# The norm of the memory tokens in two passes: row sums first with one raw tile for each block, then a second load whose rows ScalarE scales, and the norm's weight applied where the turned rows leave PSUM

## The chip, the core and the metric

One NeuronCore of a Trainium2 chip runs the whole program. The time is the device's time for one execution in microseconds (us), and of several runs the median counts. PE is TensorE (matmuls; PEld are its weight loads), ACT is ScalarE, DVE is VectorE, POOL is GpSimd, and SP is the queue of the sync engine, which here issues nearly all DMA transfers.

## The reference, cut to what matters

One encoder layer: a token mixer with two groups of attention heads, a cross-attention into 256 memory tokens, and an MLP. The part that changes is the norm of the memory tokens ahead of the cross-attention's keys and values:

```python
def rmsnorm(x, g):
    y = xf * lax.rsqrt(jnp.mean(xf * xf, axis=-1, keepdims=True) + EPS) * g
...
mem_n = rmsnorm(mem, g_mem_kv[l])          # mem: 256 x 1024
k = (mem_n @ w_mk).reshape(B, M, MEM_HEADS, MEM_HEAD_DIM)
v = (mem_n @ w_mv).reshape(B, M, MEM_HEADS, MEM_HEAD_DIM)
```

## The kernel before

Every product runs as three matmuls of split operands: an operand is cut into a high part (`hi`, rounded by an ACT copy) and a low part (`lo`, the difference, by DVE or POOL), and `mm3` (lines 193 to 195) adds hi x hi, lo x hi and hi x lo in PSUM.

The attention phase starts about 60 us into the span. A planner, the class `Flow`, writes the order of the instructions of every engine while the program is built: it keeps six streams of PE steps and queues of small jobs for ACT ("S"), DVE ("V"), POOL ("G") and SP ("D"), each with an assumed cost, and at each point takes the first stream whose next step is ready by its own clock. On the chip each engine then runs its list strictly in this order. The streams are, by priority: the value products of the heads (`pv`, line 766), the transposes of probabilities (`ptr`, line 723), the scores (`sc..`/`sf..`, lines 650 and 651), side steps, row statistics, and last the filler, which projects the q, k and v of later head pairs (n = 0 to 7; tiles `q_0`, `q_1`, `k_0`, ...). The filler of pair n+1 may start only when the tiles of an older pair are free, that is when that pair's scores are all done. So at each change of pair the filler can run out shortly before it may go on.

A unit of scores for 128 queries goes in pieces, here of 384 and 256 columns: two matmuls into one of two PSUM banks (tag `s`), then a custom DVE instruction (line 654) that adds the bias and takes the row minimum, which also frees the bank. ACT takes the exponent (line 663), POOL normalises (line 666), PE transposes, ACT and DVE split the result into `phl` (lines 732 and 729).

Weights come through a ring of three raw 128 x 1024 tiles (tag `wraw`): class `Stock` lists the blocks in the order of their use, loads one as soon as a raw tile is free, and splits it on ACT (line 461) and POOL or DVE when a place for the split weight is free. Two entries in that list belong to the memory tokens. At "norm", placed ahead of q of pair 5, `mem_norm` takes all three raw tiles: one for the norm's weight spread over 128 partitions, two for the blocks of memory rows; each block is squared and summed on ACT (line 931), its root taken on POOL (lines 934 and 935), scaled by root and weight in one DVE instruction (line 937) and stored to DRAM (`md`). At "mem", ahead of k of pair 7, `mem_loads` loads the two normed blocks again (`memn`). `side_steps` then turns them on PE in four groups of four 128 x 128 transposes (`tr_mem`), and each group leaves PSUM by one ACT copy (`mT_hi`, line 915) and one DVE subtraction (`mT_lo`, line 912). The memory's key product `mk` is the next filler.

Of the kernel before, what the change touches and what calls it, by code (L numbers as in the profile page):

```python
# [14 lines left out]
F32 = mybir.dt.float32  # L15
# [7 lines left out]
P = 128  # L23
S = 1024
# [10 lines left out]
def f(ap):  # L35
    return ap.bitcast(F32)
# [99 lines left out]
def build(ctx, tc, nc, out, t):  # L136
# [105 lines left out]
    nc.vector.memset(o1024, 1.0 / 1024.0)  # L242
    bfgt = const.tile([8, 1], F32, name="bfgt")
    gcol = const.tile([P, KC], F32, name="gcol")

    od = [[dr.tile([P, HT], F32, name=f"od{k}_{h}") for h in range(2)] for k in range(KC)]
    x1d = [dr.tile([P, D], F32, name=f"x1d{b}") for b in range(TB)]
    x2d = [dr.tile([P, D], F32, name=f"x2d{b}") for b in range(TB)]
    rd = dr.tile([8, 768], F32, name="rd")
    md = [dr.tile([P, D], F32, name=f"md{b}") for b in range(2)]  # L250
    cd = dr.tile([8, S], F32, name="cd")
    td = {k: [dr.tile([P, 2, HT], F32, name=f"{k}d{i}") for i in range(2)] for k in ("T1", "T2", "T3", "T4")}

# [121 lines left out]
    def raw_tile(name):  # L375
        return wp.tile([P, D], F32, tag="wraw", bufs=3, name=name)
# [22 lines left out]
    class Stock:  # L399
# [3 lines left out]
        def __init__(self):  # L403
            self.blocks = []
            for n, (kind, pr) in enumerate(ORDER):
                if n == 5:
                    self.blocks.append("norm")
                b = (0 if kind == "f" else 8) + pr
                self.blocks.append((("q", n), t["w_qk"][b], [P, KC, P]))
                if n > 3:  # L410
                    self.blocks.append((("v", n), t["w_v"][n - 4], [P, KC, P]))
                if n == 7:
                    self.blocks.append("mem")
                self.blocks.append((("k", n), t["w_qk"][b + 4], [P, KC, P]))
# [71 lines left out]
        def pump(self):  # L486

            while self.to_load:
                if isinstance(self.to_load[0], str):
                    n = 3 if self.to_load[0] == "norm" else 2  # L490
                    if not free["raw"].ready(n):
                        break
                    for _ in range(n):
                        free["raw"].take()
                    (mem_norm if self.to_load.pop(0) == "norm" else mem_loads)()
                    break
                if not free["raw"].ready():
                    break
                free["raw"].take()
                key = self.to_load[0][0]  # L500
                self.load()
                flow.put("D", flow.now, 0.55, lambda: None, lambda at, k=key: seen.__setitem__(("raw", k), at + 4.2))
# [370 lines left out]
    def side_steps():  # L873
# [23 lines left out]
        for k in range(0, KC, 2):  # L897
# [8 lines left out]
                    nc.tensor.transpose(tr[:, j, q, :], mem_in[q][:, (k + j) * P:(k + j + 1) * P], ident)  # L906
            src = tr.rearrange("p a q b -> p a (q b)")
            i, o = k // mT.per, k % mT.per
            dh, dl = mT.h[i][:, o:o + 2, :], mT.l[i][:, o:o + 2, :]

            def lo(at, src=src, dh=dh, dl=dl, k=k):
                flow.put("V", at, 0.7, lambda: nc.vector.tensor_sub(dl, src, f(dh)),
                         lambda end: (free["tr"].give(end), seen.__setitem__(("mT", k), end)), 1)

            flow.put("S", flow.end, 0.6, lambda src=src, dh=dh: nc.scalar.activation(dh, src, AF.Copy), lo, 1)
        for _ in range(2):
            free["raw"].give(flow.end)


    def mem_norm():  # L920

        g = raw_tile("g_mem_kv")
        nc.sync.dma_start(g, t["g_mem_kv"].to_broadcast([P, D]))
        for b in range(2):
            xt = raw_tile(f"mem{b}")
            nc.sync.dma_start(xt, t["mem"][b * P:(b + 1) * P, :])
            r, ss = (small.tile([P, 1], F32, tag=k, bufs=8, name=f"{k}_mem{b}") for k in ("rstd", "ss"))

            def square(xt=xt, ss=ss, b=b):
                junk = p1.tile([P, D], BF16, tag="phl", bufs=2, name=f"junkm{b}")  # L930
                nc.scalar.activation(junk, xt, AF.Square, scale=1.0 / 32.0, accum_out=ss)

            def root(r=r, ss=ss):
                nc.gpsimd.tensor_scalar(r, ss, EPS, None, op0=ALU.add)
                nc.gpsimd.tensor_tensor(r, r, mhalf[:, 0:1], op=ALU.pow)

            scale = lambda xt=xt, r=r: nc.vector.scalar_tensor_tensor(xt, xt, r, g, op0=ALU.mult, op1=ALU.mult)
            store = lambda xt=xt, b=b: nc.sync.dma_start(md[b], xt)
            flow.chain(flow.now + 6 + b, [("S", 1.1, square), ("G", 0.9, root), ("V", 1.3, scale), ("D", 0.55, store)],
                       lambda at, b=b: [free["raw"].give(at) for _ in range(1 + b)] and seen.__setitem__(("md", b), at))  # L940

    mem_in = []

    def mem_loads():
        for b in range(2):
            xt = raw_tile(f"memn{b}")
            nc.sync.dma_start(xt, md[b])
            mem_in.append(xt)
        seen["mem"] = flow.now + 6

    def memory_steps(keep):
        for nb in range(KC):
# [896 lines left out]
    with tc.manual_schedule():  # L1849
# [116 lines left out]
            nc.scalar.activation(rrows[:, th, :], tr.rearrange("p a b -> p (a b)"), AF.Copy)  # L1966
        nc.sync.dma_start(bfgt, t["b_fgt"])
        nc.sync.dma_start(gcol, t["g_heads"])

        def scaled(th, kc):  # L1970
            x = xT[th][kc // 2][:, kc % 2, :]
# [806 lines left out]
def _layout(i):  # L2778
    import numpy as np

    def a(x):
        return np.ascontiguousarray(np.asarray(x, dtype=np.float32) if not isinstance(x, np.ndarray) else x)
# [6 lines left out]
    def parts(w, ranges):  # L2789
# [25 lines left out]
        "w_ff2q": a(i["w_ff2"][0].reshape(2, 2, 4, 2, P, 2, 2, 256)[1].transpose(4, 2, 5, 0, 3, 1, 6).reshape(2, 4, 2, P, D)),  # L2815
        "w_ff2": a(i["w_ff2"][0].reshape(2, 8, 2, P, 2, HT).transpose(0, 4, 1, 3, 2, 5).reshape(4, 8, P, D)),
        "g_mem_pre": a(i["g_mem_pre"].reshape(KC, P).T),
        **{k: i[k] for k in ("g_mix_post", "g_mem_kv", "g_mem_post",
                             "g_ff_pre", "g_ff_post")},
    }  # L2820

# [13 lines left out]
```

## Time and profile before

| | |
|---|---|
| median of 3 runs | 1450.36 us (1448.18 to 1451.93) |
| span of the profiled execution | 1448.0 us |
| PE busy | 1436.0 us (99%) |
| PEld busy | 1223.0 us (84%) |
| DVE busy | 1127.7 us (78%) |
| ACT busy | 871.1 us (60%) |
| POOL busy | 373.9 us (26%) |
| granted TensorE clock | 1.000 over the span, its upper level of 2.4 GHz |

The span runs from the first instruction to the last; nothing else of the profiled execution's own time is recorded, and the three runs lie between 0.2 and 3.9 us above it. A matmul's busy time reaches beyond the start of the next one, since matmuls are pipelined. So an engine that is "99% busy" can hide short stalls, and they are read from the starts: in a stretch without waits a matmul over 512 columns starts 0.23 us after the one before it, over 384 columns 0.17 us, over 256 columns 0.12 us. What a start is late by those steps is a stall, whether the view counts it as idle time or not.

### The profile page before, as it was taken

Reading aid. Unit: us, or ns where it says so; the run is one execution under the profiler, and the core shown is the slowest. Engines: PE = TensorE matmul, PEld = TensorE weight load, DVE = VectorE, ACT = ScalarE, POOL = GpSimd, SP = SyncE. Lnnn points to the kernel's source line nnn. Section 1 sums busy time; section 2 is a strip of 40 time slices with the busy share of each in tenths; the row PEclk is TensorE's granted clock in tenths of the full one; section 3 lists DMA queues with packets and bytes.
Section 4 is the critical chain, followed back from the end, with each engine's and each line's share of the span. In section 5 each row is a group of like instructions: output and inputs, shape, how many; then the busy total and the mean of one; then the engine's idle time right before and its main releaser. Section 6 shows DMA issues by size and latency. Waiting matters only on the chain. (4 is left out here: it accounts for less than half of the span.)

```text
span 1448.0 us, 21869 instructions
## 1 busy us (share of the span) xinstructions
PE 1436.0 (99%) x7505; PEld 1223.0 (84%) x7505; DVE 1127.7 (78%) x1918; ACT 871.1 (60%) x1509; POOL 373.9 (26%) x472
## 2 busy tenths in 40 slices
PE   9999999999999999999999999999999999999998
PEld 8988888888889888888888888888888888888886
DVE  6788787867677856879788787996666866789897
ACT  6567676766677845885566565445555555555553
POOL 1145565645454310211113511003322000000003
PEclk9999999999999999999999999999999999999999
DMA  7143424442415585542144637775455996786785
GB/s 278 49 121 98 120 70 139 150 124 65 106 54 153 172 291 205 192 157 88 44 133 173 219 130 242 260 262 185 167 178 179 315 344 238 259 283 229 275 290 204
DMA packets 109439, 262.12 MB, mean 181 GB/s; under 512 B 12280, under 2 KB 30720, under 8 KB 109328
## 3 DMA queue, kind: packets, MB, share of 16 engines
q1 hardware_dynamic: 109184, 260.47, 54.0%
q8 instruction: 59, 0.97, 0.3%
q14 instruction: 52, 0.43, 0.1%
q10 hardware_dynamic: 144, 0.26, 0.1%
HBM read 186.70 MB, written 65.59 MB: 174 GB/s over the span
## 5 line engine op out<-in xcount | busy, mean ns | idle before, releaser
L729 DVE TENSOR_TENSOR phl<-ptr,phl 128x512 fp32r<-128x512 f32 (+1 forms) x152 | 92.3, 615 | 30.9 <-ACT phl L732 29.7
L732 ACT ACTIVATE phl<-ptr 128x512 fp32r<-128x512 f32 (+1 forms) x152 | 79.6, 539 | 49.4 <-PE ptr L723 47.7
L2471 ACT ACTIVATE whif<-ra 128x1024 fp32r<-128x1024 f32 x45 | 47.6, 1059 | 76.8 <-PE fx L194 34.8
L2606 POOL TENSOR_SCALAR rf<-sf 128x1 f32<-128x1 f32 x7 | 7.0, 1004 | 316.0 <-ACT jf L2587 315.8
L766 PE MATMUL pv<-phl,vs 128*128 128x512 f32 (+1 forms) x304 | 85.9, 367 | 0.4 <-DVE phl L729 0.4
L2473 DVE TENSOR_TENSOR wlof<-ra,whif 128x1024 fp32r<-128x1024 f32 x45 | 55.0, 1222 | 35.9 <-ACT whif L2471 35.8
L193 PE MATMUL fx<-vhif,whif 128*128 128x512 f32 x168 | 65.6, 390 | 0.0
L194 PE MATMUL fx<-vlof,whif 128*128 128x512 f32 x168 | 65.6, 390 | 0.0
L195 PE MATMUL fx<-vhif,wlof 128*128 128x512 f32 x168 | 65.4, 389 | 0.0
L766 PEld LDWEIGHTS pv<-phl,vs 128*128 128x128 f32 x304 | 54.7, 188 | 10.5 <-DVE phl L729 1.4
L780 POOL TENSOR_TENSOR o<-o 64x256 f32<-64x256 f32 x64 | 47.8, 747 | 51.8 <-DVE o L778 35.3
L2322 POOL TENSOR_TENSOR sc<-wf,wf 128x512 f32<-128x512 f32 x8 | 12.7, 1581 | 177.4 <-DMA wf<-in_w_ff 177.4
L1545 POOL TENSOR_SCALAR mp<-mp,mst 128x256 f32<-128x256 f32 x32 | 24.6, 775 | 125.1 <-DVE mst L1544 85.7
L193 PE MATMUL k<-hT_hi,whik 128*128 128x512 f32 x128 | 53.2, 416 | 0.0
L193 PE MATMUL q<-hT_hi,whiq 128*128 128x512 f32 x128 | 51.7, 404 | 0.0
L778 DVE TENSOR_TENSOR o<-pv,o 64x512 f32<-64x512 f32 x64 | 43.9, 686 | 9.7 <-ACT o L783 8.7
L193 PE MATMUL yw<-whiwo,yT_hi 128*128 128x512 f32 x128 | 50.6, 395 | 0.0
L195 PE MATMUL k<-hT_hi,wlok 128*128 128x512 f32 x128 | 50.3, 393 | 0.0
L194 PE MATMUL k<-hT_lo,whik 128*128 128x512 f32 x128 | 50.3, 393 | 0.0
L194 PE MATMUL yw<-wlowo,yT_hi 128*128 128x512 f32 x128 | 50.2, 392 | 0.0
L195 PE MATMUL q<-hT_hi,wloq 128*128 128x512 f32 x128 | 50.1, 392 | 0.0
L194 PE MATMUL q<-hT_lo,whiq 128*128 128x512 f32 x128 | 50.1, 392 | 0.0
(786 smaller groups left out, 5267.6 us busy)
## 6 DMA issues: line engine op xcount, KB each, us to landing
wg<-in_w_ff SPq DMA_DIRECT2D x48, 512.0 KB, 6.1
ra<-gd SPq DMA_DIRECT2D x40, 512.0 KB, 3.8
wf<-in_w_ff SPq DMA_DIRECT2D x38, 512.0 KB, 3.8
wi<-in_w_ff2q SPq DMA_DIRECT2D x28, 512.0 KB, 5.5
gd<-s SPq DMA_DIRECT2D x32, 256.0 KB, 2.7
gd<-g SPq DMA_DIRECT2D x25, 256.0 KB, 2.8
wrawq<-in_w_qk SPq DMA_DIRECT2D x8, 512.0 KB, 4.5
wrawk<-in_w_qk SPq DMA_DIRECT2D x8, 512.0 KB, 3.7
```

Source lines behind the costliest of these rows:

```text
L193: nc.tensor.matmul(ps, lh, rh, start=start, stop=False, skip_group_check=more)
L194: nc.tensor.matmul(ps, lh, rl, start=False, stop=False, skip_group_check=more)
L195: nc.tensor.matmul(ps, ll, rh, start=False, stop=stop, skip_group_check=more)
L729: flow.put("V", at, 0.7, lambda: nc.vector.tensor_sub(pl[:, live, :], tr[:, live, :], f(ph[:, live, :])), done)
L732: flow.put("S", flow.end, 0.6, lambda ph=ph, tr=tr, live=live: nc.scalar.activation(ph[:, live, :], tr[:, live, :], AF.Copy), split)
L766: nc.tensor.matmul(pv[:, :, qs_, :], v, hl[:, :, hs, :], start=c == 0 and turn == 0, stop=last)
L778: flow.put("V", at, 0.7, lambda: nc.vector.tensor_add(o2[own], pv[own, :, :, ::step], o2[own]), lambda end: (free["pv"].give(end), flow.pu ...
L780: free["pv"].give(end), flow.put("G", end, 0.8, lambda: nc.gpsimd.tensor_add(o2[own, 0], o2[own, 0], o2[own, 1]), store)))
L1545: mul = lambda st=st, pr=pr: nc.gpsimd.tensor_scalar(pr, pr, st[:, 2:3], 1.0, op0=ALU.mult, op1=ALU.mult)
L2322: eng.tensor_sub(sc[:, k1], r0[:, k0], r1[:, k0])
L2471: nc.scalar.activation(ah, ra, AF.Copy)
L2473: nc.vector.tensor_sub(al, ra, f(ah))
```

## The change

The "norm" entry stands twice in the list, ahead of q of pairs 4 and 5, and takes one raw tile each time. Such an entry loads one block of memory rows, squares it in place on ACT with the row sums going to a column of a small constant tile `rkv`, and takes the root there on POOL. The DVE multiplication, the load of the spread weight and the stores to `md` are gone. At "mem" both blocks are loaded again from the input, and ACT scales each in place by its root column. The weight is loaded as 128 x 8 columns (`gkv`) near the start. When turned rows leave PSUM, memory channels lie on partitions, so the weight is a column there: each group of transposes now leaves in two halves, each by an ACT copy scaled by a weight column and a DVE `scalar_tensor_tensor` with the same column, 128 x 256 apiece.

```diff
             for n, (kind, pr) in enumerate(ORDER):
-                if n == 5:
+                if n in (4, 5):
                     self.blocks.append("norm")
...
-                    n = 3 if self.to_load[0] == "norm" else 2
+                    n = 1 if self.to_load[0] == "norm" else 2
...
-            dh, dl = mT.h[i][:, o:o + 2, :], mT.l[i][:, o:o + 2, :]
-
-            def lo(at, src=src, dh=dh, dl=dl, k=k):
-                flow.put("V", at, 0.7, lambda: nc.vector.tensor_sub(dl, src, f(dh)),
-                         lambda end: (free["tr"].give(end), seen.__setitem__(("mT", k), end)), 1)
-
-            flow.put("S", flow.end, 0.6, lambda src=src, dh=dh: nc.scalar.activation(dh, src, AF.Copy), lo, 1)
+            turned = all_of(("mT", k), 2, free["tr"].give)
+            for j in range(2):
+                x, g = src[:, j, :], gkv[:, k + j:k + j + 1]
+                dh, dl = mT.h[i][:, o + j, :], mT.l[i][:, o + j, :]
+                flow.put("S", flow.end, 0.4, lambda x=x, g=g, dh=dh: nc.scalar.activation(dh, x, AF.Copy, scale=g),
+                         lambda at, x=x, g=g, dh=dh, dl=dl, turned=turned: flow.put(
+                             "V", at, 0.42, lambda: nc.vector.scalar_tensor_tensor(
+                                 dl, x, g, f(dh), op0=ALU.mult, op1=ALU.subtract), turned, 1), 1)
...
-        g = raw_tile("g_mem_kv")
-        nc.sync.dma_start(g, t["g_mem_kv"].to_broadcast([P, D]))
-        for b in range(2):
-            xt = raw_tile(f"mem{b}")
-            nc.sync.dma_start(xt, t["mem"][b * P:(b + 1) * P, :])
...
-            scale = lambda xt=xt, r=r: nc.vector.scalar_tensor_tensor(xt, xt, r, g, op0=ALU.mult, op1=ALU.mult)
-            store = lambda xt=xt, b=b: nc.sync.dma_start(md[b], xt)
...
+        xt = raw_tile(f"mem{b}")
+        nc.sync.dma_start(xt, t["mem"][b * P:(b + 1) * P, :])
+        r = rkv[:, b:b + 1]
...
+        square = lambda: nc.scalar.activation(xt, xt, AF.Square, scale=1.0 / 32.0, accum_out=r)
+        flow.put("S", flow.now + 6, 1.1, square, lambda at: (
+            free["raw"].give(at), flow.put("G", at, 0.9, root, mark(("rkv", b)))), 1)
...
-            nc.sync.dma_start(xt, md[b])
+            nc.sync.dma_start(xt, t["mem"][b * P:(b + 1) * P, :])
             mem_in.append(xt)
-        seen["mem"] = flow.now + 6
+            flow.put("S", flow.now + 6, 1.1, lambda xt=xt, b=b: nc.scalar.activation(
+                xt, xt, AF.Copy, scale=rkv[:, b:b + 1]), both, 1)
```

PE runs the same 7204 rows as before, but the planner places some of them elsewhere: its order is the same up to the middle of q of pair 2 (about 136 us in the trace of before), differs from there to the last scores of heads `f7` (a block or two also just ahead of `mk`), and is the same from `mk` to the end. Three places follow.

ScalarE, during the scores of heads `c2`, before:

```order
L663 ACTIVATE spc2g_1584,smc2g_1600<-spc2g_1584,mnc2g_1589 128x512
L783 ACTIVATE o_1631<-pv_1554 64x512
L732 ACTIVATE phl_1638<-ptr_1637 128x512
L663 ACTIVATE spc2g_1611,smc2g_1625<-spc2g_1611,mnc2g_1601 128x640
L732 ACTIVATE phl_1663<-ptr_1662 128x384
```

ScalarE at the same place of the change (its lines count one more):

```order
L664 ACTIVATE spc2g_1585,smc2g_1601<-spc2g_1585,mnc2g_1590 128x512
L784 ACTIVATE o_1632<-pv_1555 64x512
L936 ACTIVATE mem_1553,rkv<-mem_1553 128x1024
L733 ACTIVATE phl_1639<-ptr_1638 128x512
L664 ACTIVATE spc2g_1612,smc2g_1626<-spc2g_1612,mnc2g_1602 128x640
L733 ACTIVATE phl_1667<-ptr_1666 128x384
```

The first square of memory rows now stands between an eviction of head outputs and the copy of a group of turned probabilities.

TensorE at the end of the scores of `c2`, just before k of pair 2 (`k_0`) may start, before:

```order
L193 MATMUL q_1_1605<-hT_hi_154,whiq_1249 128x512
L194 MATMUL q_1_1605<-hT_lo_158,whiq_1249 128x512
L195 MATMUL q_1_1605<-hT_hi_154,wloq_1250 128x512
L766 MATMUL pv_1728<-phl_1689,vs_0_182 128x512
L766 MATMUL pv_1728<-phl_1689,vs_0_182 128x2x128
L650 MATMUL sc2g_1734<-kd_1290,qs_1046 128x384
L651 MATMUL sc2g_1734<-kl_1291,qs_1046 128x384
L723 MATMUL ptr_1738<-ident,spc2g_1584 128x128 x3
L650 MATMUL sc2g_1745<-kd_1290,qs_1046 128x256
L651 MATMUL sc2g_1745<-kl_1291,qs_1046 128x256
L193 MATMUL k_0_1751<-hT_hi_143,whik_1506 128x512
```

TensorE there in the change:

```order
L724 MATMUL ptr_1705<-ident,spc2g_1559 128x128 x3
L724 MATMUL ptr_1711<-ident,spc2g_1585 128x128 x4
L651 MATMUL sc2g_1720<-kd_1291,qs_1047 128x384
L652 MATMUL sc2g_1720<-kl_1292,qs_1047 128x384
L651 MATMUL sc2g_1725<-kd_1291,qs_1047 128x256
L652 MATMUL sc2g_1725<-kl_1292,qs_1047 128x256
L651 MATMUL sc2g_1736<-kd_1291,qs_1047 128x384
L652 MATMUL sc2g_1736<-kl_1292,qs_1047 128x384
L651 MATMUL sc2g_1746<-kd_1291,qs_1047 128x256
L652 MATMUL sc2g_1746<-kl_1292,qs_1047 128x256
L193 MATMUL k_0_1751<-hT_hi_143,whik_1507 128x512
```

Four score pieces for two banks now follow one another with nothing between them, where projections, value products and transposes stood between them; the last three matmuls of q of pair 2 have gone ahead of them.

TensorE at the next change of pair, from k of pair 2 to q of pair 3, before:

```order
L650 MATMUL sc3g_1998<-kd_1292,qs_1047 128x384
L651 MATMUL sc3g_1998<-kl_1293,qs_1047 128x384
L650 MATMUL sc3g_2005<-kd_1292,qs_1047 128x256
L651 MATMUL sc3g_2005<-kl_1293,qs_1047 128x256
L193 MATMUL k_1_1863<-hT_hi_154,whik_1506 128x512
L194 MATMUL k_1_1863<-hT_lo_158,whik_1506 128x512
L195 MATMUL k_1_1863<-hT_hi_154,wlok_1507 128x512
L650 MATMUL sc3g_2020<-kd_1292,qs_1047 128x384
L651 MATMUL sc3g_2020<-kl_1293,qs_1047 128x384
L650 MATMUL sc3g_2029<-kd_1292,qs_1047 128x256
L651 MATMUL sc3g_2029<-kl_1293,qs_1047 128x256
L193 MATMUL q_0_2036<-hT_hi_143,whiq_1795 128x512
```

TensorE there in the change:

```order
L651 MATMUL sc3g_1988<-kd_1293,qs_1048 128x384
L652 MATMUL sc3g_1988<-kl_1294,qs_1048 128x384
L651 MATMUL sc3g_1992<-kd_1293,qs_1048 128x256
L652 MATMUL sc3g_1992<-kl_1294,qs_1048 128x256
L651 MATMUL sc3g_2008<-kd_1293,qs_1048 128x384
L652 MATMUL sc3g_2008<-kl_1294,qs_1048 128x384
L651 MATMUL sc3g_2013<-kd_1293,qs_1048 128x256
L652 MATMUL sc3g_2013<-kl_1294,qs_1048 128x256
L767 MATMUL pv_1957<-phl_1974,vs_3_185 128x512
L767 MATMUL pv_1957<-phl_1974,vs_3_185 128x2x128
L651 MATMUL sc3g_2028<-kd_1293,qs_1048 128x384
L652 MATMUL sc3g_2028<-kl_1294,qs_1048 128x384
```

The three matmuls of `k_1` that stood between the second and the third piece have gone ahead here too, and after the four pieces two more follow with only value products and transposes between them.

## Rows read from the trace of the kernel before

**Rows 1.** The page's first part: busy time, share, instructions.

```profile
PE 1436.0 (99%) x7505; PEld 1223.0 (84%) x7505; DVE 1127.7 (78%) x1918; ACT 871.1 (60%) x1509; POOL 373.9 (26%) x472
```

**Rows 2.** Windows: stretch, its length, each engine's busy time, clock, DMA share.

```profile
60.00:512.00 452.00, 451.08 (x2498) 385.70 (x2497) 348.25 (x866) 316.13 (x626) 224.97 (x321) 1.00 0.40 116
1000.00:1025.00 25.00, 25.00 (x112) 20.71 (x111) 21.11 (x27) 13.47 (x20) 5.84 (x4) 1.00 0.63 208
```

**Rows 3.** PE's waits from 60 to 512 us: total, times, longest.

```profile
PE pv L766 <- DVE phl L729: 0.4, 2, 0.2
PE sc3g L650 <- DVE mnc3g L654: 0.2, 1, 0.2
PE mk L193 <- DVE km_lo L969: 0.2, 1, 0.2
```

**Rows 4.** PE's timeline around the old norm: start, length, instruction.

```profile
256.45 0.40 PE L194 MATMUL k<-hT_lo,whik 128*128 128x512 f32 x1
256.68 0.40 PE L195 MATMUL k<-hT_hi,wlok 128*128 128x512 f32 x1
257.23 0.52 PE L723 MATMUL ptr<-ident,spf2g 128*128 128x128 f32 x3
...
266.21 0.40 PE L195 MATMUL k<-hT_hi,wlok 128*128 128x512 f32 x1
266.79 0.73 PE L766 MATMUL pv<-phl,vs 128*128 128x512 f32 x2 [0.19 <-DVE phl L729]
```

**Rows 5.** DVE's timeline around the old norm.

```profile
250.03 1.28 DVE L937 SCALAR_TENSOR_TENSOR mem<-mem,rstd_mem,g_mem_kv 128x1024 f32<-128x1024 f32 x1
...
253.98 2.63 DVE L937 SCALAR_TENSOR_TENSOR mem<-mem,rstd_mem,g_mem_kv 128x1024 f32<-128x1024 f32 x1
256.53 0.55 DVE L729 TENSOR_TENSOR phl<-ptr,phl 128x384 fp32r<-128x384 f32 x1
```

**Rows 6.** Timeline of all engines at the change from k to q.

```profile
159.02 0.54 DVE L654 CUSTOM_DVE_ANT_0 spc3g<-sc3g,biasc 128x384 f32<-128x384 f32 x1
...
159.36 0.40 PE L195 MATMUL k<-hT_hi,wlok 128*128 128x512 f32 x1
...
159.63 0.45 PE L650 MATMUL sc3g<-kd,qs 128*128 128x384 f32 x1
...
159.91 0.34 PE L651 MATMUL sc3g<-kl,qs 128*128 128x384 f32 x1
...
159.97 0.47 DVE L654 CUSTOM_DVE_ANT_0 spc3g<-sc3g,biasc,mnc3g 128x256 f32<-128x256 f32 x1
...
160.50 0.39 PE L650 MATMUL sc3g<-kd,qs 128*128 128x256 f32 x1 [0.25 <-DVE mnc3g L654]
```

**Rows 7.** Timeline of all engines where k of pair 2 starts.

```profile
139.54 0.39 PE L195 MATMUL k<-hT_hi,wlok 128*128 128x512 f32 x1
...
139.92 0.33 PE L650 MATMUL sc3g<-kd,qs 128*128 128x128 f32 x1
```

**Rows 8.** Single instructions by tile: count, least/median/greatest ns, first and last start.

```profile
L931 ACT ACTIVATE junkm<-mem x2: 1052/1056/1060, 246.0 to 249.0; 128x1024 bf16<-128x1024 f32 x2
L355 ACT ACTIVATE vs<-v x8: 366/380/397, 47.0 to 57.5; 128x256 fp32r<-128x256 f32 x8
L1359 ACT ACTIVATE h2r<-tr_h2T,gmem x32: 464/484/519, 590.6 to 639.9; 128x256 f32<-128x256 f32 x32
L353 DVE SCALAR_TENSOR_TENSOR vs<-v,rx,vs x8: 471/484/485, 26.5 to 39.9; 128x256 fp32r<-128x256 f32 x8
L915 ACT ACTIVATE mT_hi<-tr_mem x4: 597/598/599, 435.2 to 445.3; 128x512 fp32r<-128x512 f32 x4
L912 DVE TENSOR_TENSOR mT_lo<-tr_mem,mT_hi x4: 692/692/692, 435.8 to 446.0; 128x512 fp32r<-128x512 f32 x4
```

**Rows 9.** ACT's timeline where the first square now stands.

```profile
130.00 0.59 ACT L783 ACTIVATE o<-pv 64x512 f32<-64x512 f32 x1 [0.58 <-issue]
131.14 0.60 ACT L732 ACTIVATE phl<-ptr 128x512 fp32r<-128x512 f32 x1 [0.55 <-PE ptr L723]
```

**Rows 10.** Weights of q of pair 4: load issued (SP), split (ACT), used (PE).

```profile
124.78 0.34 SPq L446 DMA_DIRECT2D wrawq<-in_w_qk  x1
...
186.22 1.05 ACT L461 ACTIVATE whiq<-wrawq 128x1024 fp32r<-128x1024 f32 x1
...
203.89 0.40 PE L193 MATMUL q<-hT_hi,whiq 128*128 128x512 f32 x1
```

**Rows 11.** PE's first product of the turned memory rows.

```profile
448.02 0.28 PE L193 MATMUL mk<-mT_hi,whimk 128*128 128x256 f32 x1
```

More of the change, by code (lines that the diff above doesn't have):

```diff
@@ L244, in build @@
     gcol = const.tile([P, KC], F32, name="gcol")
+    gkv = const.tile([P, KC], F32, name="gkv")
+    rkv = const.tile([P, 2], F32, name="rkv")
     od = [[dr.tile([P, HT], F32, name=f"od{k}_{h}") for h in range(2)] for k in range(KC)]
@@ L249, in build @@
     rd = dr.tile([8, 768], F32, name="rd")
-    md = [dr.tile([P, D], F32, name=f"md{b}") for b in range(2)]
     cd = dr.tile([8, S], F32, name="cd")
@@ L916, in side_steps @@
         for _ in range(2):
             free["raw"].give(flow.end)
+    normed_mem = []
     def mem_norm():
-        g = raw_tile("g_mem_kv")
-        nc.sync.dma_start(g, t["g_mem_kv"].to_broadcast([P, D]))
-        for b in range(2):
-            xt = raw_tile(f"mem{b}")
-            nc.sync.dma_start(xt, t["mem"][b * P:(b + 1) * P, :])
[L927 to L935, printed above, removed]
-            scale = lambda xt=xt, r=r: nc.vector.scalar_tensor_tensor(xt, xt, r, g, op0=ALU.mult, op1=ALU.mult)
-            store = lambda xt=xt, b=b: nc.sync.dma_start(md[b], xt)
-            flow.chain(flow.now + 6 + b, [("S", 1.1, square), ("G", 0.9, root), ("V", 1.3, scale), ("D", 0.55, store)],
-                       lambda at, b=b: [free["raw"].give(at) for _ in range(1 + b)] and seen.__setitem__(("md", b), at))
@@ new lines, in mem_norm, with root @@
+        b = len(normed_mem)
+        normed_mem.append(b)
+        xt = raw_tile(f"mem{b}")
+        nc.sync.dma_start(xt, t["mem"][b * P:(b + 1) * P, :])
+        r = rkv[:, b:b + 1]
+        def root():
+            nc.gpsimd.tensor_scalar(r, r, EPS, None, op0=ALU.add)
+            nc.gpsimd.tensor_tensor(r, r, mhalf[:, 0:1], op=ALU.pow)
+        square = lambda: nc.scalar.activation(xt, xt, AF.Square, scale=1.0 / 32.0, accum_out=r)
+        flow.put("S", flow.now + 6, 1.1, square, lambda at: (
+            free["raw"].give(at), flow.put("G", at, 0.9, root, mark(("rkv", b)))), 1)
@@ L942, in build @@
     mem_in = []
     def mem_loads():
+        both = all_of("mem", 2)
         for b in range(2):
             xt = raw_tile(f"memn{b}")
-            nc.sync.dma_start(xt, md[b])
+            nc.sync.dma_start(xt, t["mem"][b * P:(b + 1) * P, :])
             mem_in.append(xt)
-        seen["mem"] = flow.now + 6
+            flow.put("S", flow.now + 6, 1.1, lambda xt=xt, b=b: nc.scalar.activation(
+                xt, xt, AF.Copy, scale=rkv[:, b:b + 1]), both, 1)
     def memory_steps(keep):
@@ L1968, in build @@
         nc.sync.dma_start(gcol, t["g_heads"])
+        nc.sync.dma_start(gkv, t["g_mem_kv"])
         def scaled(th, kc):
@@ L2817, in _layout @@
         "g_mem_pre": a(i["g_mem_pre"].reshape(KC, P).T),
-        **{k: i[k] for k in ("g_mix_post", "g_mem_kv", "g_mem_post",
+        "g_mem_kv": a(i["g_mem_kv"].reshape(KC, P).T),
+        **{k: i[k] for k in ("g_mix_post", "g_mem_post",
                              "g_ff_pre", "g_ff_post")},
```

## The prediction

> **What bounds the kernel now.** I read the page's first part first: TensorE is busy 1436.0 of 1448.0 us, no other engine over 78% [rows 1]. The next question is whether the stretch that the change touches has stalls to give back. The windows say hardly any: from 60 to 512 us PE is idle for 452.00 - 451.08 = 0.92 us [rows 2], and the list of PE's waits there holds 0.8 us, all on DVE [rows 3]. Those numbers are too low, since a matmul's busy time covers the start of the next, so I went to the timeline and read starts. After the 512-column matmul at 256.68 the next starts at 257.23, 0.55 us later instead of 0.23, a stall of 0.32 us that no view counts; at 266.21 it is 0.58 instead of 0.23, a stall of 0.35 [rows 4]. At the changes of pair it is 139.92 - 139.54 - 0.23 = 0.15 us [rows 7], and near 160 us two late starts: 159.91 - 159.63 = 0.28 where 0.17 is the step, and 160.50 - 159.91 = 0.59 where 0.17 is the step, together 0.53 us [rows 6]. So the kernel is bound by the number of PE's instructions, which the change leaves alone; what it can move is these stalls of tenths of a microsecond. The clock was 1.00 in both windows, its upper level [rows 2], and since PE nowhere pauses for long I expect it to stay there.
>
> A rule of the Trainium skill would see it otherwise. "Perfetto Trace Analysis", section "Identifying the Most-Contended Engine", says that the busy share of matmuls doesn't show how near TensorE is to its roofline, and that the busy share of weight loads does; here that is 84%, which would leave 16%. The trace doesn't let me read that as room: in the stretch from 1000 to 1025 us, where PE has no idle time, 112 matmuls started in 25 us, one in 0.223 us, and the loads were busy 20.71 of 25 us, 83% [rows 2]. By the rule the sum below would be a minor part of what could be won; by the row 83 to 85% is what a full PE looks like, and I go by the row.
>
> **The change part by part.** *Gone from DVE:* two multiplications of the memory rows, 1.28 and 2.63 us [rows 5]. The second one held up the subtraction of `phl` behind it until 256.53, and PE's stall at 256.68 ends after that. That stall of 0.32 us goes. The one at 266.21 also waits for a `phl`, but ten microseconds later; the new order may or may not have it. Bounds for the gain: 0.32 to 0.67 us; I take 0.5, the middle, because the rows say nothing on the second.
>
> *Gone from SP:* one spread load, two stores. *Added to SP:* the small load of `gkv`, where the queue is ahead of need. These cost PE nothing; the cover is the weight ring, which works far ahead: q of pair 4 was loaded at 124.78, split at 186.22 and used at 203.89 [rows 10]. The first new memory load takes that load's raw tile and gives it back after the square, so q of pair 4 comes one landing and one square later, out of 61 us of slack before the split. If that cover were gone, the price would be in the rivals.
>
> *The squares:* each 1.06 us on ACT as before [rows 8], but in other places. The first stands between the instructions at 130.00 and 131.14 [rows 9], where ACT had 0.55 us free. So the copy of `phl` behind it comes some 1.06 - 0.55 = 0.5 us later, and the value products and DVE's subtraction behind that too. PE doesn't wait there, because the planner gives it filler of q of pair 2 instead. That filler is missing at the next change of pair, and this is where I see the cost. In the new order four score pieces for two banks stand in a row; the third can't start before DVE has read the first, nor the fourth before DVE has read the second.
>
> What does such a row of four cost? The kernel before has nearly this at 160 us, with one block of three matmuls (3 x 0.23 = 0.69 us) between the second and the third piece, and still lost 0.53 us [rows 6]. Without the block the third piece would have come 0.69 us sooner but DVE's reading at 159.02 and 159.97 would not, so the row of four costs 0.53 + 0.69 = 1.22 us. *At k of pair 2* the stall was 0.15 us [rows 7] and becomes 1.22: +1.07. *At q of pair 3* it was 0.53 and becomes 1.22: +0.69. Bounds: if DVE reads the pieces at once, the third waits only for one reading (0.54 us) less what PE has between, so nearly nothing: 0 at both places. If a `phl` subtraction (0.55 us) stands ahead of each second reading, each row of four costs 0.55 more: +1.62 and +1.24; the two further pieces at the second place can add one more reading, 0.47 us. I take the middle values, since the old row of four is nearest. The second square, ahead of q of pair 5, falls where a whole pair of projections is at hand as filler: 0, and up to 0.5 if it delays ACT as the first one does.
>
> *The second load and its scaling:* two copies of 128 x 1024 with a column. The trace has none; a square of that size takes 1.06 us, and a column adds 0.484 - 0.380 = 0.10 us to a copy of 256 columns [rows 8], so 1.06 to 1.2 us each. They stand before 400 us, and the transposes that read the result run at 434: 0. Here a rule speaks against the change. "ScalarE: Activation LUTs", section "Rules for kernel authors", wants multiplications on VectorE, not ScalarE. For these operands the rows price it the other way: 1.28 us or more on DVE [rows 5] against 1.06 to 1.2 on ACT. As neither engine is the bound, the sum is the same by both.
>
> *The evictions of the turned rows:* before, four copies of 0.598 us and four subtractions of 0.692 us; after, eight scaled copies of 0.484 us and eight `scalar_tensor_tensor` of 0.484 us, by the same forms elsewhere in the kernel [rows 8]. ACT gets 3.87 - 2.39 = 1.48 us more, DVE 3.87 - 2.77 = 1.10 us more, between 435 and 447 us. The last `mT_lo` began at 446.0 [rows 8] and `mk` needs it for its seventh of eight channel blocks: three 256-column matmuls a block, 6 x 3 x 0.12 = 2.2 us after 448.02 [rows 11], so about 3.5 us after it was ready. The last group grows by 2 x 0.484 + 0.484 - 0.598 - 0.692 = 0.16 us. Covered: 0. Without cover it would cost the 1.1 us of DVE; half of that, 0.5 us, is my upper bound, for `phl` splits delayed in the same stretch.
>
> **Sum:** -0.5 + 1.07 + 0.69 = +1.26 us. Against the profiled execution that is 1448.0 + 1.3 = 1449.3 us of span; the median of the runs lay 2.36 us above that span, so the time is 1450.36 + 1.26 = 1451.6 us. Low end of the costs: -0.67 + 0 + 0 = -0.7, so 1449.7. High end: -0.32 + 1.62 + 1.24 + 0.47 + 0.5 + 0.5 = +4.0, so 1454.4. The three runs spread by 3.75 us, half of which, 1.9 us, a median of a few runs can be off by on the low side. The likeliest case's own range is 1449.7 to 1454.4.
>
> **The rivals.** *Small gain:* freeing 3.9 us of DVE time [rows 5] and the raw ring lets the planner's new order run with fewer stalls than the old one, and the rows of four are hidden. For it: all waits of PE in this stretch are on DVE [rows 3]. Against: all stalls read above come to 0.32 + 0.35 + 0.15 + 0.53 = 1.35 us, and no more can be won than is lost. Time: 1449.0 to 1450.3, say 1449.7. It is no measurable change either.
>
> *Slower beyond measure:* the squares sit in ACT's fixed order, each behind a load that SP issues some 6 us earlier. Should a memory block land late, everything behind the square waits: `phl`, exponents, copies of k. The ring's load before it was issued at 124.78 and ACT would reach the square at 130.6 [rows 9, 10]. It decides from a landing of more than 5.8 us; each microsecond beyond is lost on ACT, and PE feels it once its filler is gone. To lose over 0.3% (4.35 us) with the +1.26 of the sum it takes 3.1 us more over both squares, landings of about 7.4 us each. Time then: 1450.36 + 1.26 + 3.1 = 1454.7 or more, say 1456.
>
> *PE has room after all:* if PE were not full between 60 and 512 us, where its loads were busy 385.70 of 452 us [rows 2], a tenth of the 66 us of difference would make it 6.6 us faster: 1443.8. By the Trainium skill's rule on loads this could be; the row at 1000 us speaks against it.
>
> **How the numbers follow.** Forecast (0 to +4 us, likeliest +1.26): 0.62. Small gain: 0.25. Slower beyond measure, by the late load or longer rows of stalls: 0.10. Room on PE: 0.03. Within 0.3% (1446.0 to 1454.7, about what a measurement of this kernel can tell from no change) lie the first two: 0.87; slower 0.10; faster 0.03. The range goes from the small gain less the spread of the runs, 1449.7 - 1.9 = 1447.8, to just beyond the high end of the costs, 1454.8: 7 us, and about 1 in 10 is left out.
>
> **What would show it.** Right: PE's count and the 0.23 us step unchanged; between about 137 and 141 us, and 158 and 163 us, score matmuls that start 0.3 to 0.7 us late and wait for DVE's reading; no late start near the old norm; `mk` starting without a wait; two squares of 1.06 us directly behind what precedes them on ACT. Wrong: a square that waits for a DMA; a projection that waits for its weights; late starts near 435 to 450 us that wait for `mT_lo` or `phl`; or a span that moved by more than the stalls add up to, which I would not understand.

## The result: slightly slower, by two rows of score pieces

The changed kernel takes 1453.31 us (median of 12 runs, 1451.70 to 1454.72), the kernel before on the same chip 1449.49 us (12 runs): a ratio of 1.0026, with a 95% interval of 1.0017 to 1.0034. That is 3.8 us more: above zero by its interval, and less than the 0.3% that the prediction took for the limit of what can be told from no change; with twelve runs of each kernel it can be told. The forecast was 1451.6 us. The page's first part of the changed kernel, whose profiled span is 1452.0 us (4.0 more than before):

```profile
PE 1437.4 (99%) x7505; PEld 1223.1 (84%) x7505; DVE 1121.6 (77%) x1920; ACT 875.9 (60%) x1515; POOL 373.2 (26%) x472
```

PE's instructions are the same 7505 as in [rows 1], so the 4 us are no added work: they are waits, and in one place slower matmuls. PE's waits from 60 to 512 us (total, times, longest), against [rows 3]:

```profile
PE sc3g L651 <- DVE mnc3g L655: 2.0, 2, 1.6
PE sc2g L651 <- DVE mnc2g L655: 1.0, 2, 0.7
PE tr_mem L907 <- DVE mT_lo L916: 0.2, 1, 0.2
PE pv L767 <- DVE phl L730: 0.2, 1, 0.2
```

Two lines are new in size: score pieces that wait for DVE's reading of the piece two before. (Lines of the changed kernel count one more than those of before.) They are the two rows of four that the order shows. PE's timeline at the first, just before k of pair 2:

```profile
136.93 0.28 PE L651 MATMUL sc2g<-kd,qs 128*128 128x256 f32 x1
137.05 0.28 PE L652 MATMUL sc2g<-kl,qs 128*128 128x256 f32 x1
138.03 0.45 PE L651 MATMUL sc2g<-kd,qs 128*128 128x384 f32 x1 [0.71 <-DVE mnc2g L655]
138.32 0.34 PE L652 MATMUL sc2g<-kl,qs 128*128 128x384 f32 x1
138.90 0.39 PE L651 MATMUL sc2g<-kd,qs 128*128 128x256 f32 x1 [0.25 <-DVE mnc2g L655]
```

Read by starts, as in the prediction: the third piece comes 138.03 - 137.05 - 0.12 = 0.86 us late, the fourth 138.90 - 138.32 - 0.17 = 0.41 us, together 1.27 us. On DVE an addition of head outputs (`o`) stands ahead of the first reading and a subtraction of `phl` ahead of the second:

```profile
136.69 0.69 DVE L779 TENSOR_TENSOR o<-pv,o 64x512 f32<-64x512 f32 x1 [0.69 <-ACT o L784]
137.41 0.56 DVE L655 CUSTOM_DVE_ANT_0 spc2g<-sc2g,biasc 128x384 f32<-128x384 f32 x1
137.90 0.55 DVE L730 TENSOR_TENSOR phl<-ptr,phl 128x384 fp32r<-128x384 f32 x1
```

PE's timeline at the second row, from k of pair 2 to q of pair 3:

```profile
158.42 0.28 PE L651 MATMUL sc3g<-kd,qs 128*128 128x256 f32 x1
158.53 0.28 PE L652 MATMUL sc3g<-kl,qs 128*128 128x256 f32 x1
160.45 0.44 PE L651 MATMUL sc3g<-kd,qs 128*128 128x384 f32 x1 [1.64 <-DVE mnc3g L655]
...
161.56 0.62 PE L767 MATMUL pv<-phl,vs 128*128 128x512 f32 x2
162.50 0.69 PE L651 MATMUL sc3g<-kd,qs 128*128 128x384 f32 x1 [0.32 <-DVE mnc3g L655]
162.98 0.52 PE L652 MATMUL sc3g<-kl,qs 128*128 128x384 f32 x1
...
163.94 1.70 PE L724 MATMUL ptr<-ident,spc3g 128*128 128x128 f32 x7
165.29 0.49 PE L651 MATMUL sc3g<-kd,qs 128*128 128x256 f32 x1
```

The third piece is 160.45 - 158.53 - 0.12 = 1.80 us late, and a later one 162.50 - 161.56 - 2 x 0.23 = 0.48. Then matmuls that wait for nothing run slowly: seven transposes take 165.29 - 163.94 = 1.35 us. The windows there say why (stretch, length, busy time of each engine, clock, DMA share, GB/s):

```profile
157.80:160.40 2.60, 1.02 (x8) 0.81 (x6) 1.94 (x4) 2.38 (x4) 0.12 (x1) 1.00 0.92 275
160.40:163.00 2.60, 2.21 (x8) 1.40 (x9) 2.31 (x9) 1.52 (x3) 2.39 (x2) 0.83 0.38 92
163.00:165.60 2.60, 2.60 (x12) 2.50 (x11) 1.89 (x8) 2.02 (x4) 1.78 (x2) 0.51 0.62 195
```

PE was busy 1.02 of 2.60 us, and behind that the granted clock fell to about half, its lower level of 1.2 GHz, for some 3 us.

What held the third piece is seen on ACT and DVE:

```profile
157.15 1.21 ACT L860 ACTIVATE kd<-k 64x512 fp32r<-64x512 f32 x2 [2.11 <-PE k L195]
158.39 1.41 DVE L861 TENSOR_TENSOR kl<-k,kd 64x512 fp32r<-64x512 f32 x2 [3.15 <-ACT kd L860]
159.83 0.56 DVE L655 CUSTOM_DVE_ANT_0 spc3g<-sc3g,biasc 128x384 f32<-128x384 f32 x1
```

Two subtractions that split the new k stand ahead of the first reading, and had waited for ACT's copies of k. Those could start only when k's last matmul, which starts at 156.73, was done.

To compare kernels over longer stretches I took for every PE instruction how much later the next one starts than is usual (the median) behind an instruction of that shape, and added these up. From before to after the sum goes from 0.85 to 2.06 us at 100 to 150 us, from 1.42 to 4.94 at 150 to 200, from 1.42 to 0.78 at 250 to 300, from 0.64 to 1.02 at 400 to 450, and over the span from 21.8 to 26.0. This difference, 4.2 us, is that of the spans, 4.0.

### The profile page after: what moved, and what is told of

It is laid out like the page before. It is cut to its first block, busy times and chain, and to the rows that moved or that the text cites. A ratio compares the mean times of both kernels' runs of the same rounds, so it can differ in the third digit from the quotient of the medians.

```text
span 1452.0 us, 21885 instructions
## 1 busy us (share of the span) xinstructions
PE 1437.4 (99%) x7505; PEld 1223.1 (84%) x7505; DVE 1121.6 (77%) x1920; ACT 875.9 (60%) x1515; POOL 373.2 (26%) x472
## 4 chain that ended last, share of the span: by engine, by line
PE 92%; DVE 5%; issue 1%; ACT 1%; DMA 1%; SPq 0%; DVEq 0%; ACTq 0%
PE pv L767 4%; PE fx L194 4%; PE fx L193 4%; PE fx L195 4%; PE ptr L724 4%; PE px L195 3%; PE px L194 3%; PE px L193 3%; PE yw L193 2%; PE q L193 2%; PE yw L194 2%; PE q L195 2%; PE q L194 2%; PE k L193 2%; PE yw L195 2%; PE k L195 2%
```

## The experiments

The theory: the loss is in the order that the planner writes once it has counted a square of 1.1 us on ACT ahead of q of pair 4, and not in any work that was added. The rivals: the square or its load itself; the raw tiles; the evictions in halves and the second load. Each ratio is against the kernel before on the same chip, with a 95% interval. "After" is the changed kernel.

**e1_late.** After, but:

```diff
-                if n in (4, 5):
-                    self.blocks.append("norm")
+                if n == 5:
+                    self.blocks += ["norm"] * 2
```

> The changed kernel, with both first passes of the norm entered ahead of q of pair 5 and none ahead of q of pair 4. On TensorE the order up to pair 4 is then that of the kernel before, with no row of four score pieces. Theory (the loss is the two rows of four, 1.2 us of stalls more at 100 to 150 us and 3.5 us more at 150 to 200 us than before): 1453.3 - 1.2 - 3.5 = 1448.6 us, a ratio of 0.9994 to the kernel before, no wait of sc2g or sc3g pieces for DVE at 137 and 160 us, and a granted clock of 1.00 throughout 130:165. Rival (the loss is in what every position keeps, the evictions in halves, the second load and the scale on ACT): 1452 to 1453.5 us.

Measured: 1448.49 us (before 1448.93), ratio 0.9995 (0.9987 to 1.0004). The late starts are 0.92 us at 100 to 150 and 1.45 at 150 to 200, as before the change; no sc2g wait is left and 0.2 us of sc3g waits, as in [rows 3]; the clock was 1.00 from 130 to 165 us. All else of the change is in this kernel, so all else together costs nothing that can be measured.

**e2_after_q.** After, with both entries a block later than its first one:

```diff
-                if n in (4, 5):
-                    self.blocks.append("norm")
...
+                if n == 4:
+                    self.blocks += ["norm"] * 2
                 if n > 3:
                     self.blocks.append((("v", n), t["w_v"][n - 4], [P, KC, P]))
```

> The changed kernel, with both first passes of the norm entered between q and v of pair 4: one weight block later than the first of the changed kernel, and the second one earlier than a whole pair. TensorE's order has no row of four score pieces. Theory (the rows of four are the loss, and early loads in themselves cost nothing): 1447.0 to 1449.0 us. Rival (two raw tiles taken early hold up the weights of pair 4, and the loss comes from late weights): 1453 us or more, with new waits of TensorE for weights of v or k of pair 4.

Measured: 1449.16 us, ratio 1.0000 (0.9991 to 1.0009), 0.16 us above the range expected. From 150 to 200 us the late starts fall to 0.71 us, but at 200 to 250 they rise to 1.03 (after: 0.56) and at 400 to 450 to 1.24. PE waits for no weights between 150 and 520 us, so the rival falls: the raw tiles don't matter. Another order has its waits in other places.

**e3_order.** After, with the first pass of memory block 0 only counted:

```diff
+        if b == 0:
+            none = lambda: None
+            flow.put("S", flow.now + 6, 1.1, none, lambda at: (
+                free["raw"].give(at), flow.put("G", at, 0.9, none, mark(("rkv", b)))), 1)
+            return
...
-                xt, xt, AF.Copy, scale=rkv[:, b:b + 1]), both, 1)
+                xt, xt, AF.Copy, scale=rkv[:, 1:2]), both, 1)
```

> The changed kernel in its exact order on TensorE and VectorE, but the first pass of memory block 0 is left out: one load, one square on ScalarE and two small GpSimd operations do not run, while the planner still counts them (block 0 is scaled by block 1's root, so its rows are wrong). Theory (the order alone is the loss): 1453.3 us within 0.7, the same rows of four with a stall near 1.8 us at 158 to 160 us and a clock near half in the 3 us behind it. Rival (the square's 1.06 us in ScalarE's line, or its load, is the loss): 1449 to 1450 us.

Measured: 1451.80 us, ratio 1.0024 (1.0015 to 1.0033). One load, one square and two small GpSimd operations are gone, and the loss stays. But the clock did not fall in the profiled execution; a window and two starts:

```profile
163.00:165.60 2.60, 2.60 (x18) 2.33 (x17) 2.57 (x11) 2.46 (x6) 1.80 (x3) 1.00 0.64 181
```

```profile
158.51 0.28 PE L652 MATMUL sc3g<-kl,qs 128*128 128x256 f32 x1
160.43 0.44 PE L651 MATMUL sc3g<-kd,qs 128*128 128x384 f32 x1 [1.64 <-DVE mnc3g L655]
```

The wait is the same 1.80 us. From the second row's first piece to the first matmul of q it took 164.83 - 157.97 = 6.86 us, in the changed kernel's profile 166.20 - 157.99 = 8.21: the fall of the clock cost 1.35 us there. That part of the expectation missed, and the median is 0.8 us below the range expected.

**e4_untold.** After, with the same work in the same place, which the planner doesn't count:

```diff
-        flow.put("S", flow.now + 6, 1.1, square, lambda at: (
+        flow.put("S", flow.now + 6, 1.1 if b else 0.0, square, lambda at: (
```

> The changed kernel with the same first pass at the same place, ahead of q of pair 4, but the planner counts its square as 0 us, so that TensorE's order up to pair 4 is again that of the kernel before, with no row of four. Theory (order is the loss, the square itself is free): 1448.6 to 1449.5 us. Rival (the work itself is the loss): 1451 to 1453.5 us, with phl copies 1.06 us late at 130 us and a stall of TensorE behind them.

Measured: 1448.07 us (before 1448.93), ratio 0.9994 (0.9985 to 1.0003), 0.5 us below the range expected. ACT's timeline has the square in the place that the change gives it, between the two instructions of [rows 9]:

```profile
130.31 0.59 ACT L784 ACTIVATE o<-pv 64x512 f32<-64x512 f32 x1 [0.58 <-issue]
130.92 1.06 ACT L936 ACTIVATE mem<-mem 128x1024 f32<-128x1024 f32 x1
...
131.98 0.58 ACT L733 ACTIVATE phl<-ptr 128x512 fp32r<-128x512 f32 x1
```

It waits for no load and delays a `phl` copy, and PE's late starts from 100 to 150 us stay at 0.88 us. So the same square costs nothing that can be measured when the planner's order is the old one up to there. The raw tile and GpSimd's root are still counted in this run, so it is the 1.1 us counted on ACT that moves the filler.

**e5_no_kl.** After, with the two subtractions ahead of the reading gone from DVE:

```diff
+                    if (n, th) == (2, 1):
+                        lo = lambda l=l, own=own, cs=cs: nc.gpsimd.memset(f(l[own, cs]), 0.0)
```

> The changed kernel in its exact order on TensorE, but the low part of the second half of k of pair 2 is left out: two subtractions of VectorE, 1.41 us together, that stand ahead of the first reading of the second row of four, give way to two GpSimd memsets, so the scores of that pair lose their low part there. Theory (the second row of four lost so much because these two subtractions, late behind ScalarE's copies of k, stand ahead of the reading): the third piece of that row starts about 1.3 us earlier, its stall falls from 1.8 to about 0.5 us, and the time to 1453.3 - 1.3 = 1452.0 us or, where the clock no longer falls behind it, to 1450.7 us. Rival (four pieces for two banks cost this much in any case, by the readings and the value products behind them): the stall stays at 1.5 us or more and the time at 1453 us.

Measured: 1451.77 us (before 1449.24), ratio 1.0018 (1.0009 to 1.0027). PE's timeline:

```profile
158.84 0.28 PE L652 MATMUL sc3g<-kl,qs 128*128 128x256 f32 x1
159.54 0.45 PE L651 MATMUL sc3g<-kd,qs 128*128 128x384 f32 x1 [0.42 <-DVE mnc3g L655]
...
163.27 0.28 PE L652 MATMUL sc3g<-kl,qs 128*128 128x256 f32 x1
164.26 0.50 PE L651 MATMUL sf0g<-kd,qs 128*128 128x512 f32 x1 [0.71 <-DVE mnc3g L655]
```

The third piece waits 0.58 us instead of 1.80, as expected. But 164.26 - 163.27 - 0.12 = 0.87 us is given back at a new wait, and from the first piece to q it is 164.83 - 158.29 = 6.54 us, only 0.32 less than in e3_order. So the two subtractions set where the wait stands; without them another one comes. The time met the expectation, but not by the 1.3 us of stall, of which all but 0.32 came back; the clock was at 1.00 through this stretch. The new wait was for DVE's reading again, behind a subtraction of two SBUF operands (`B12q` and `B11q`) that took 1.57 us here. DVE and POOL in e5_no_kl:

```profile
162.16 1.57 DVE L1181 TENSOR_TENSOR B11q<-B12q,B11q 128x512 f32<-128x512 f32 x1
160.65 2.53 POOL L471 TENSOR_TENSOR wlok<-wrawk,whik 128x512 fp32r<-128x512 f32 x2 [3.09 <-ACT whik L462]
```

In e9_after, the changed kernel once more:

```profile
163.48 0.68 DVE L1179 TENSOR_TENSOR B11q<-B12q,B11q 128x512 f32<-128x512 f32 x1
160.69 2.52 POOL L471 TENSOR_TENSOR wlok<-wrawk,whik 128x512 fp32r<-128x512 f32 x2 [4.07 <-ACT whik L462]
```

In e5_no_kl POOL's pair of subtractions ended at 163.18, and DVE's subtraction 0.55 us later; in e9_after DVE's starts only when POOL's pair is over, and takes 0.68 us. The Trainium skill, "SBUF — State Buffer", section "Who interferes with whom", says that a DVE instruction with two SBUF inputs contends with a GpSimd instruction that reads SBUF, and calls the ports that they share an exclusive lock. These rows agree, 1.57 against 0.68 us. So do the two multiplications of the same size in [rows 5]: beside the first, of 1.28 us, a POOL operation took 1.29 us that takes 0.29 us at 252.66, and the second, of 2.63 us, has POOL at work in its first 1.5 us. POOL in the kernel before, beside the first:

```profile
250.17 1.29 POOL L612 TENSOR_SCALAR_AFFINE_SELECT biasf<-biasf 128x128 f32<-128x128 f32 x1
```

**e6_fill.** After, with work for PE in the wait:

```diff
+                        if (n, a, i, j) == (1, 1, 6, 0):
+                            fill = mm_tile([P, P], "fill")
+                            for _ in range(14):
+                                nc.tensor.transpose(fill, ident, ident)
                         ps = mm_tile([P, HT], f"s{nm}{j}", "s")
```

> The changed kernel with 14 transposes of the identity, whose result nobody reads, put on TensorE ahead of the third piece of the second row of four, where it waits about 1.8 us: 14 x 0.11 = 1.5 us of work inside the wait. Theory (the clock falls because TensorE stands nearly idle in this wait, and that is the part of the loss behind the wait): the granted clock stays at 1.00 from 160 to 168 us, the wait itself stays, and the time is 1453.3 us less nothing to 1.35 us, so 1452.0 to 1453.3 us. Rival (the clock falls there whatever TensorE does, or the filling delays the pieces): a clock near 0.5 in the profile, or 1454 us and more.

Measured: 1451.76 us, ratio 1.0018 (1.0009 to 1.0027), 0.24 us below the range expected. PE's timeline:

```profile
158.87 0.28 PE L656 MATMUL sc3g<-kl,qs 128*128 128x256 f32 x1
158.99 1.69 PE L652 MATMUL fill<-ident 128*128 128x128 f32 x14
160.79 0.45 PE L655 MATMUL sc3g<-kd,qs 128*128 128x384 f32 x1
...
165.18 0.40 PE L193 MATMUL q<-hT_hi,whiq 128*128 128x512 f32 x1
```

The third piece starts 1.92 us after the second as ever, the clock stays at 1.00 from 160 to 168 us, and the stretch lasts 165.18 - 158.32 = 6.86 us. No wait is listed at the third piece any more, though nothing was won: filled time looks busy.

**e7_whole.** e1_late with the evictions of before, the norm's weight left out:

```diff
-            for j in range(2):
...
+            dh, dl = mT.h[i][:, o:o + 2, :], mT.l[i][:, o:o + 2, :]
...
+            flow.put("S", flow.end, 0.6, lambda src=src, dh=dh: nc.scalar.activation(dh, src, AF.Copy), lo, 1)
```

> The kernel of e1_late with each group of turned memory rows leaving in one copy and one subtraction as before the change; the norm's weight is left out (so memory keys and values lack it). Theory (the evictions in halves hold a PSUM bank longer, which is the new stall of 0.37 us ahead of a group of tr_mem near 436 us): that stall is gone, and the time is 1448.5 - 0.4 = 1448.1 us, no measurable difference. Rival (the stall comes from the other work of the engines there): it stays.

Measured: 1448.20 us, ratio 0.9990 (0.9981 to 1.0000). PE in e1_late, and then in e7_whole:

```profile
434.97 0.49 PE L724 MATMUL ptr<-ident,spc5g 128*128 128x128 f32 x3
435.67 0.63 PE L907 MATMUL tr_mem<-ident,memn 128*128 128x128 f32 x4 [0.21 <-DVE mT_lo L916]
```

```profile
434.96 0.49 PE L724 MATMUL ptr<-ident,spc5g 128*128 128x128 f32 x3
435.28 0.60 PE L907 MATMUL tr_mem<-ident,memn 128*128 128x128 f32 x4
```

The group starts 0.70 us after the transposes with halves and 0.32 us without, so the halves cost 0.38 us, once. The group waited for DVE's `mT_lo` of an earlier group, which frees its PSUM bank.

**e8_before_nomul.** Before, without the old norm's multiplications:

```diff
-            scale = lambda xt=xt, r=r: nc.vector.scalar_tensor_tensor(xt, xt, r, g, op0=ALU.mult, op1=ALU.mult)
+            scale = lambda: None
```

> The kernel before, in its exact order, without the two multiplications of memory rows on VectorE (1.28 and 2.63 us; the memory rows stay unnormed). Theory (the second one held up a subtraction of phl, and TensorE behind it): the late start of 0.32 us behind the matmul at 256.7 us is gone; of the one of 0.35 us at 266.2 us, ten microseconds later, the rows said nothing, and it goes too if it belongs to the same delay. Time 1448.9 less 0.3 to 0.7, so 1448.2 to 1448.6 us. Rival (these late starts have another cause): both stay, 1448.9 us.

Measured: 1448.75 us (before 1449.24), ratio 1.0000 (0.9990 to 1.0009). PE at the two places of [rows 4]:

```profile
256.06 0.40 PE L195 MATMUL k<-hT_hi,wlok 128*128 128x512 f32 x1
256.30 0.49 PE L723 MATMUL ptr<-ident,spf2g 128*128 128x128 f32 x3
```

```profile
265.24 0.40 PE L195 MATMUL k<-hT_hi,wlok 128*128 128x512 f32 x1
265.73 0.73 PE L766 MATMUL pv<-phl,vs 128*128 128x512 f32 x2
```

The first late start is gone (0.24 us, the usual step); of the second 0.26 of 0.35 us stays. So the multiplications cost about 0.4 us in the old order, and the time can't tell.

**e9_after and e10_fill.** The changed kernel and e6_fill once more, unaltered, side by side.

> The changed kernel once more, unaltered, beside the next one on the same chip. Theory (the fall of the clock behind the wait at 160 us is part of the change's cost and not of one execution only): the window 163 to 166 us shows a clock near 0.5 again, and the median lies 0.7 to 1.4 us above that of e10_fill. Rival (the fall was the chance of one execution, as the same wait without it in e3_order says): a clock of 1.00, and medians that agree within 0.5 us.

> The kernel of e6_fill once more, beside the changed kernel on the same chip. Theory: clock 1.00 throughout 155:170 again, median 0.7 to 1.4 us below that of e9_after. Rival: within 0.5 us of it.

Measured (before 1449.20): e9_after 1452.36 us, ratio 1.0023 (1.0014 to 1.0032); e10_fill 1451.86 us, ratio 1.0019 (1.0010 to 1.0028). In e9_after the wait is there in full and the clock is 1.00:

```profile
158.94 0.28 PE L652 MATMUL sc3g<-kl,qs 128*128 128x256 f32 x1
160.86 0.45 PE L651 MATMUL sc3g<-kd,qs 128*128 128x384 f32 x1 [1.64 <-DVE mnc3g L655]
...
165.25 0.39 PE L193 MATMUL q<-hT_hi,whiq 128*128 128x512 f32 x1
```

Here 165.25 - 158.39 = 6.86 us, and the late starts from 150 to 200 us are 3.61 us instead of 4.94. In e10_fill the clock is 1.00 from 155 to 170 us. The medians lie 0.5 us apart, at the edge of the rival's range and below the theory's. So one and the same kernel has the fall in one execution and not in another. The mean clock of every run, kept to three digits, hints at how often: of the eleven runs of e9_after five show 0.998 and took 1452.66 to 1453.50 us, six show 0.999 and took 1451.58 to 1452.36 us; all eleven of e10_fill show 0.999. That fits a fall in about half of the executions that costs some 1.1 us. It is no proof: five of the 22 runs of the kernel before beside them show 0.998 too, and are no longer than the others.

**e11_before_gap.** Before, with the planner counting what isn't there:

```diff
+                if n == 4:
+                    self.blocks.append("gap")
...
+                    flow.put("S", flow.now + 6, 1.1, none, lambda at: (
+                        free["raw"].give(at), flow.put("G", at, 0.9, none)), 1)
```

> The kernel before with nothing of the change but its order: ahead of q of pair 4 the planner counts one raw tile, 1.1 us of ScalarE and 0.9 us of GpSimd, for which no instruction runs. TensorE's order gets the same two rows of four, and every instruction is that of the kernel before, the old norm included. Theory (these rows are the whole loss): 1.2 us more stall at 100 to 150 us and 2.2 us at 150 to 200 us (3.5 where the clock falls), so 1449.2 + 3.4 = 1452.6 us, to 1453.9 us with the clock, a ratio of 1.0023 to 1.0033. Rival (part of the loss is the new norm's own work): 1450.5 us or less.

Measured: 1453.74 us (6 runs), ratio 1.0030 (1.0019 to 1.0042). The first row of four begins at 136.50, its third piece at 138.04, 0.01 us from the changed kernel's; the second row's third piece is 1.78 us late. The clock fell, and the stretch from the second row's first piece to q lasted 165.95 - 157.98 = 7.97 us. A window behind the wait:

```profile
163.00:165.60 2.60, 2.60 (x14) 2.50 (x13) 1.88 (x8) 2.13 (x6) 1.79 (x2) 0.60 0.61 205
```

Against the kernel before, the late starts rise by 1.2 us at 100 to 150 us and by 3.3 us at 150 to 200, as the theory has it with the fall of the clock. So the loss, in its whole size, comes about in the kernel before as well, with no instruction of the change, once its order has the two rows.

## Why the prediction was right, and where its sizes were off

*Bound and clock.* PE's count did not change, nor did its steps where the clock was at 1.00, and 4.0 us of span are 4.2 us of late starts. "I expect it to stay there" was wrong of the clock: behind a wait of 1.8 us it fell in two of the four profiles that have this wait unfilled (the changed kernel and e11_before_gap; not in e3_order and e9_after), and in neither with the wait filled. Where it fell it cost 1.35 us in the changed kernel and 7.97 - 6.86 = 1.11 us in e11_before_gap.

*Gone from DVE.* Forecast -0.5 (bounds -0.67 to -0.32). The late starts from 250 to 300 us fell by 1.42 - 0.78 = 0.64 us. Of this e8_before_nomul gives some 0.4 to the multiplications; where the rest comes from is not shown. The late start at 266.2 us, on which the prediction's rows said nothing, has little to do with the old norm: in the trace of before, DVE's `phl` there stands behind a subtraction of two SBUF operands (`B22q` and `B12q`) that took 1.91 us from 264.04.

*The row of four at k of pair 2.* Forecast 1.22 us, measured 1.27; the late starts from 100 to 150 us rose by 1.21 where the forecast had 1.07. Mechanism and size were right. The size fits because DVE had the same work here as at the old row, an `o` addition ahead of the first reading and a `phl` subtraction ahead of the second, which the prediction did not look at. DVE in the kernel before, ahead of the reading at 159.02 of [rows 6]:

```profile
158.41 0.68 DVE L778 TENSOR_TENSOR o<-pv,o 64x512 f32<-64x512 f32 x1 [0.57 <-ACT o L783]
```


*The row of four at q of pair 3.* This is the term that was mis-sized: 0.53 "becomes 1.22: +0.69". Measured are 1.80 us at the third piece alone, and 3.61 - 1.42 = 2.19 us more of late starts without the fall of the clock, 4.94 - 1.42 = 3.52 with it. Both lie above the prediction's own upper bounds for this place, 1.24 + 0.47 = 1.71 us, and of the late starts that it named as a sign, 0.3 to 0.7 us each, those measured at the two rows are 0.86, 0.41 and 1.80 us. The step that failed is taking the old row as the nearest, since there nothing of the new k stands ahead of DVE's reading at 159.02 [rows 6]. In the new order k's last three matmuls go ahead of the row, so ACT's copies and DVE's subtractions of the new k (1.41 us) come ahead of the first reading; my bound had one `phl` subtraction of 0.55 us, ahead of the second reading. e5_no_kl adds that this is not all of it: with these gone the stretch is 0.32 us shorter, as PE has no filler there and meets DVE again a few pieces later.

*The squares.* That they cost through the order and not through ACT's time was right: e3_order keeps the loss without the first square, e4_untold keeps the square without the loss. The second square cost nothing that shows.

*The second load and its scaling:* two copies of 1.14 us (1.06 to 1.2 forecast) in good time, as e1_late shows with all of it in place. *The evictions:* 0.480 us for each `scalar_tensor_tensor` (0.484 forecast), and 0.38 us of PE's time, within the bound of 0.5. But the forecast was 0, and a late start near 435 to 450 us that waits for `mT_lo` was one of the signs of being wrong; this one came. The cover was worked out for the last group and `mk`, while the wait came between two groups, for the bank (e7_whole).

*The sum.* -0.64 + 1.21 + 2.19 + 0.38 = +3.1 us, and +4.5 with the fall of the clock. The second comparison measured 1452.36 - 1449.20 = 3.2 us, the first 3.8. Forecast was +1.26, and the high end +4.0 for the likeliest case. That 1453.31 us lies within the range is in part luck: the forecast's base, a median of three runs, lies 0.9 us above that of twelve, and the excess at q of pair 3 was taken up by bounds of other terms that were not needed (0.5 for the second square, 0.4 at k of pair 2).

*The rivals.* Small gain: not with the planner's order, though e1_late (-0.4 us) and e4_untold (-0.9 us) point there, within what can be told from nothing. Slower by a late load: the square waited for no load. Room on PE: nothing points to it; where waits went, in e1_late and e4_untold, the time came back to that of before and not clearly below it.

## What to carry to other kernels

Where a planner writes the order, price a change by the order that it brings and not by its instructions alone: here 1.1 us that ran beside other work cost nothing, but counted in a queue it moved the filler away from two places, for 3.4 us. In such a place, read what stands on the reading engine ahead of the release, and from when that can run; here, removing one item (e5_no_kl) only brought the next one up. The cheapest mend here was one list entry placed elsewhere (e1_late), which undid the loss and left the rest of the change in place.

## What the runs showed of the hardware that was not expected

The clock of TensorE can fall to its lower level behind a single wait of 1.8 us, in a stretch in which PE was busy 1.02 of 2.60 us; it came back within some 3 us. The same wait, to 0.02 us, left the clock at 1.00 in other executions, of the same kernel too (in e3_order PE was busy 0.99 us of the same 2.60), so a single profile can't price it. A subtraction on DVE whose operands both lie in SBUF took 1.57 us beside POOL's subtractions and 0.68 us right after them.
